# Every second forward substitution on POOL, and the two heads of a pair alternating in scores and chunk products

## The chip, the cores and the metric

The kernel runs on one core of a Trainium2 chip. Its engines are TensorE (PE: matrix products, PEld its weight loads), VectorE (DVE), ScalarE (ACT), GpSimd (POOL) and SyncE (SP), which here only issues transfers. Each engine takes its own instructions in the order in which the program put them down; between engines, semaphores make an instruction wait for what it reads and for buffers to come free. The metric is the device time of one execution in microseconds (us), lower is better; an execution with a profile gives the trace.

## The reference

One inference step of a hybrid decoder layer, for a prompt of 512 positions and, with the same weights, 8 single-token samples with caches. All is float32, the model width is 1024.

```python
proj = h @ w_in                        # h: RMS norm of x
# attention: 3 groups of 8 heads of 64, windows (128,1) (512,4) (2048,16): rotary q, k,
#   scores of 128-row blocks against 128 or 256 keys, masked softmax, times v,
#   groups weighted by the softmax of their log-sum-exp -> o_a
# RWKV-7 time mixing: 16 heads of 64, state S (64 x 64) carried over the 512 positions
def step(S, inp):
    r_t, w_t, k_t, v_t, kk_t, a_t = inp
    sa = einsum('bhij,bhj->bhi', S, -kk_t)
    S = S * w_t + sa * (kk_t * a_t) + v_t * k_t
    return S, einsum('bhij,bhj->bhi', S, r_t)
# group norm, bonus, gate -> o_b
merged = sigmoid(gate_a) * (o_a @ w_proj_a) + sigmoid(gate_b) * (o_b @ w_proj_b)
x = x + merged @ w_out
x = x + (silu(hn @ w_gate) * (hn @ w_up)) @ w_down
y = rms_norm(x)
```

The outputs are y for prompt and samples, the new keys and values, the new shift columns and the new states.

## The kernel before

**Layout and main stream.** Columns are the 512 prompt positions and the 8 samples, 520 in all, computed in two parts of 260. Every dense projection is a list of output tiles of 128 rows; a weight tile is split into a high and a low part (`whi` by ScalarE, `wlo` by VectorE), and each step of the inner dimension is three products, high times high, low times high and high times low, into a bank of accumulators called `mm` (three buffers). The main stream plays these tiles in the order input projections, gates, `w_proj_a`, `w_proj_b`, `w_out`, gate and up, down.

**Side work.** Beside it run generators, which the program calls the weave: attention `heads(g)` for each group, and for each of the eight pairs of RWKV heads `pair(p)`, `solve(p)`, a turn, `chain(p)`, `back(p)`. They take their accumulators from three buffers `ax` (`bank()`) and two single ones `ch0` and `ch1` (`cbank(i)`). `BANK` and `CBANK(i)` give the moment at which the next of them is expected to be free. A generator yields what must be ready before it can go on, and flags (`wv.set`, `wv.until`) order generators among each other.

**What sets the order.** The order is fixed when the program is built. `Clocks` keeps a planned time for each engine, and `Unit.price` gives each instruction a price: for VectorE 0.07 us plus n/960, for POOL 0.25 us plus n/480, where n is the number of elements per partition; a dependent instruction on the same engine starts 0.12 us later. Whenever the planned clock has passed what a generator waits for, its next piece is put into the engines' queues, otherwise dense tiles are. Every recorded instruction stands at line 380, the call in `Unit`, so the profile is read by tile names.

**Scores.** `heads(g)` goes through four pairs of heads. A pair's queries and keys lie in one tile, the first head in partitions 0 to 63, the second in 64 to 127. Before, the first head's blocks are multiplied into one `ch` bank after the other, each bank emptied by VectorE into `sm`, and then the second head's.

**Chunk products.** `pair(p)` cuts the 512 positions into 8 chunks of 64 and multiplies, for each head, the stacked tiles `BK` and `AR` of a chunk (contraction over the 64 rows of that head). Four chunks of one head fill an `ax` bank, VectorE multiplies it with a mask into `GH`, and in the second half POOL scales a part of it with `DN`.

**Forward substitution.** `solve(p)` inverts the unit triangular 32 by 32 blocks of a pair: two transfers bring them into `LT` (128 x 31 x 32), `Xs` (tile `X`, 128 x 8 x 32) starts as ones on the diagonal, and then there are 31 steps of two instructions, `xt = X * LT` and `X = X + xt`, in which the number of elements goes from 31 up to 76 and down to 8. `LT` and `X` have two buffers (`SOLVERS`), `xt` has one; every three steps (`SOLVE`) the generator yields. Two more transfers take the result back into `GH`, products on TensorE complete it to blocks of 64, and the flag `solved` lets the turn and the chain of that pair go on. The chain of pair p writes the state `o_wkvp` and gives `back(p)` what it needs for the tile `OB` that `w_proj_b` reads. `pb_pre(n)` and `pb_post(n)` are what goes before and after tile n of that projection.

Of the kernel before, what the change touches and what calls it, by code (L numbers as in the profile page):

```python
# [8 lines left out]
FP = mybir.dt.float32  # L9
# [3 lines left out]
ALU = mybir.AluOpType  # L13
# [12 lines left out]
NP = HB // 2  # L26
# [195 lines left out]
def _bc(ap, shape):  # L222
    return ap.to_broadcast(shape)
# [86 lines left out]
class Pool:  # L310
# [10 lines left out]
        h.append(t.name)  # L321
        return t

    def next(self, tag, bufs):

        h = self.hist.get(tag, ())
        return self.ck.free(h[-bufs], "PE") if len(h) >= bufs else 0.0


class Unit:  # L330
# [135 lines left out]
def program(tc, I, O):  # L466
    nc = tc.nc
    ck = Clocks()
    V, S, G, SY = (Unit(n, e, tc, ck) for n, e in (("DVE", nc.vector), ("ACT", nc.scalar), ("POOL", nc.gpsimd), ("SP", nc.sync)))

    E = Unit("PE", nc.tensor, tc, ck, tc.keep_in_program_order if PIN else None)
# [5 lines left out]
    def nm(s):  # L477
        uid[0] += 1
        return f"{s}_{uid[0]}"
# [16 lines left out]
    def bank():  # L496
        return axp.tile([128, 512], FP, name=nm("ax"), tag="ax", bufs=3)

    def cbank(i):
        return chp.tile([128, 512], FP, name=nm("ch"), tag=f"ch{i % 2}")  # L500

    def BANK():
        return axp.next("ax", 3)

    def CBANK(i):
        return lambda: chp.next(f"ch{i % 2}", 1)
# [310 lines left out]
    def heads(g):  # L817
# [2 lines left out]
        nb = 7 if g == 0 else 4  # L820
        kw = 256 if g == 0 else 128
        per = 512 // kw
        nb_ = 0
        for hp in range(4):
            for i in range(2):
                yield from wv.until("qk", g, i, hp)
            yield from wv.until("vt", g, hp)
            yield Q[hp], K[hp]
            PT = bp.tile([128, 2, 7, 128], FP, name=nm("PT"), tag="PT")
            sms = []  # L830
            for h2 in range(2):
                h = 2 * hp + h2
                r0 = h2 * 64
                q, k = Q[hp][r0:r0 + 64], K[hp][r0:r0 + 64]
                sm = bp.tile([128, 4, kw], FP, name=nm("sm"), tag="sm", bufs=2)
                nmx = bp.tile([128, 4], FP, name=nm("nmx"), tag="nmx", bufs=4)
                for b0 in range(0, 4, per):
                    nb_ += 1
                    yield (CBANK(nb_),)
                    ps = cbank(nb_)  # L840
                    for b in range(b0, b0 + per):
                        o = (b - b0) * kw
                        qb = q[:, b * 128:b * 128 + 128]
                        if g:
                            E.matmul(ps[:, o:o + 128], lhsT=qb, rhs=k[:, b * 128:b * 128 + 128], start=True, stop=True)
                        elif b:
                            E.matmul(ps[:, o:o + 256], lhsT=qb, rhs=k[:, (b - 1) * 128:(b + 1) * 128], start=True, stop=True)
                        else:
                            E.matmul(ps[:, o + 128:o + 256], lhsT=qb, rhs=k[:, 0:128], start=True, stop=True)
                    for b in range(b0, b0 + per):  # L850
                        o = (b - b0) * kw
                        lo = 128 if g == 0 and b == 0 else 0
                        m0 = (lo, 256, 384)[g]
                        V.tensor_tensor_reduce(out=sm[:, b, lo:], in0=ps[:, o + lo:o + kw],
                                               in1=amask[:, m0:m0 + kw - lo], scale=1.0, scalar=-3.0e38,
                                               op0=ALU.add, op1=ALU.max, accum_out=stat[:, g, 0, b, h:h + 1])
                V.tensor_scalar_mul(out=nmx[:], in0=stat[:, g, 0, :, h], scalar1=-0.125)
                for b in range(4):
                    lo = 128 if (g == 0 and b == 0) else 0
                    S.activation(out=sm[:, b, lo:], in_=sm[:, b, lo:], func=AF.Exp, scale=0.125,  # L860
                                 bias=nmx[:, b:b + 1], accum_out=stat[:, g, 1, b, h:h + 1])
                sms.append(sm)
            blks = ([(0, 128)] + [(b, o) for b in range(1, 4) for o in (0, 128)]) if g == 0 else \
                [(b, 0) for b in range(4)]
            for h2 in range(2):
# [266 lines left out]
    def pair(p):  # L1132
# [73 lines left out]

        GH = [r2.tile([128, NC, 2 * C], FP, name=nm("GH"), tag=tag, bufs=4) for tag in ("GB", "GK")]
        for c0 in range(0, NC, 4):
            for h in range(2):
                yield (BANK,)  # L1210
                ps = bank()
                for c in range(c0, c0 + 4):
                    E.matmul(ps[:, (c - c0) * 128:(c - c0 + 1) * 128], lhsT=BK[H[h], c, h:h + 2].rearrange("p a t -> p (a t)"),
                             rhs=AR[H[h], :, c], start=True, stop=True)
                V.tensor_tensor(out=GH[h][:, c0:c0 + 4], in0=ps[:].rearrange("p (c x) -> p c x", c=4),
                                in1=_bc(wmask[:].unsqueeze(1), [128, 4, 128]), op=ALU.mult)
                if c0:
                    G.tensor_tensor(out=GH[h][H[h], :, 0:C], in0=GH[h][H[h], :, 0:C],
                                    in1=_bc(DN[H[h]].unsqueeze(2), [64, NC, C]), op=ALU.mult)
# [54 lines left out]

    def solve(p):
        r2, QI, GH = rw["r2"], rw["QI"], rw["GH", p]
        TD = drp.tile([4, NC, 32, 32], FP, name=nm("TD"))
        TE = drp.tile([4, NC, 32, 32], FP, name=nm("TE"))
        for q in range(4):
# [4 lines left out]

        LT = r2.tile([128, 31, 32], FP, name=nm("LT"), tag="LT", bufs=SOLVERS)
        Xs = r2.tile([128, 8, 32], FP, name=nm("X"), tag="X", bufs=SOLVERS)
        V.memset(Xs[:], 0.0)
        for a in range(4):
            V.memset(Xs[a * 32:a * 32 + 32].rearrange("p m t -> p (m t)")[:, a:256:36], 1.0)
        yield (TD,)  # L1290
        for a in range(4):
            SY.dma_start(out=LT[a * 32:a * 32 + 32], in_=TD[:, :, :31].rearrange("q c s t -> (q c) s t"))
# [1 line left out]
        for s in range(31):  # L1294
            m = s // 4 + 1
            w = 31 - s
            t = r2.tile([128, 128], FP, name=nm("xt"), tag="xt")
            tv = t[:, :m * w].rearrange("p (m w) -> p m w", m=m)
            V.tensor_tensor(out=tv, in0=_bc(Xs[:, :m, s:s + 1], [128, m, w]),
                            in1=_bc(LT[:, s:s + 1, s + 1:], [128, m, w]), op=ALU.mult)  # L1300
            V.tensor_tensor(out=Xs[:, :m, s + 1:], in0=Xs[:, :m, s + 1:], in1=tv, op=ALU.add)
            if s % SOLVE == SOLVE - 1:
                yield (Xs,)
        yield (Xs,)
# [384 lines left out]
    def pb_pre(n):  # L1689
        def pre():  # L1690
            if n == 0:
                yield from wv.until("ob", NP - 3)
                hctx.close()
                mp = mrg["pool"] = pool("mg", mctx, side="right")
                mrg["h"] = mp.tile([128, KD, NT], FR, name="mh")
                mrg["l"] = mp.tile([128, KD, NT], FR, name="ml")
            gb = gp_.tile([128, NT], FP, name=nm("gb"), tag="g", bufs=2)
            ta = full("tmp", 2)
            G.dma_start(out=gb[:], in_=GD[:, KD + n])
            G.dma_start(out=ta[:], in_=TAD[:, n])  # L1700
            mrg[n] = gb, ta
            yield ()
        return pre
# [264 lines left out]
```

## Time and profile before

| | before |
|---|---|
| median of 3 runs | 1312.92 us (1310.77 to 1315.44) |
| the profiled execution | 1316.53 us, span 1314.8 us |
| mean granted TensorE clock | 0.983 |
| busy: TensorE, VectorE, ScalarE, POOL | 1264.7, 843.7, 610.6, 175.0 us |
| instructions: TensorE, VectorE, ScalarE, POOL | 11738, 2221, 1554, 261 |
| the substitutions' 496 instructions on VectorE | 60.3 + 57.6 us |
| first and last of them | 383.6 and 745.3 us |

A row of groups reads: line, engine, operation, output and inputs by tile names, shape and count, then the busy time, the mean of one in ns, and the idle time of the engine just before, with what ended it. A float32 product of the scores or chunks shows as two records of TensorE. A row of the windows view has a stretch, its length, the busy time of each engine with the number of instructions, then the granted TensorE clock, the share of the transfer engines and GB/s.

### The profile page before, as it was taken

How to read it: one execution, taken by the hardware profiler on the slowest of the kernel's cores; microseconds unless marked ns; L12 is line 12 of the kernel's file. 1: busy time of each engine (PE TensorE's matmuls, PEld its weight loads, DVE VectorE, ACT ScalarE, POOL GpSimd, SP SyncE). 2: the span in 40 equal slices, each digit the busy share in tenths (PEclk: the TensorE clock that was granted, in tenths of full speed). 3: DMA queues.
4: the chain of work that ended last, by engine and by line, in shares of the span. 5: the costliest groups of instructions: out<-in, count | busy, mean ns of one | idle time of the engine just before them, and what ended most of it. 6: DMA issues, size and time to landing. Idle time of an engine off the chain costs nothing.

```text
span 1314.8 us, 29468 instructions
## 1 busy us (share of the span) xinstructions
PE 1264.7 (96%) x11738; PEld 1197.5 (91%) x11738; DVE 843.7 (64%) x2221; ACT 610.6 (46%) x1554; POOL 175.0 (13%) x261
## 2 busy tenths in 40 slices
PE   7999999999989989999999999999999999999996
PEld 7998999989978878888888888999999999999996
DVE  6956866954869998886986665555843444332333
ACT  5244244366656656675785665334433232222220
POOL 1300100100223332121123122110200000000000
PEclk9999999999989999997999999999999999999998
DMA  6523654634245554543245454552222222223331
GB/s 215 158 94 96 213 178 146 221 112 172 69 131 136 152 147 141 143 156 97 77 139 168 123 175 157 182 192 85 81 97 97 97 89 89 97 93 89 89 101 65
DMA packets 92137, 169.48 MB, mean 129 GB/s; under 512 B 42416, under 2 KB 47568, under 8 KB 92000
## 3 DMA queue, kind: packets, MB, share of 16 engines
q1 hardware_dynamic: 60880, 102.46, 24.6%
q0 software_dynamic: 14512, 46.47, 11.5%
q10 hardware_dynamic: 16608, 18.68, 4.3%
q8 instruction: 92, 1.51, 0.5%
q14 instruction: 45, 0.37, 0.1%
HBM read 133.20 MB, written 27.94 MB: 123 GB/s over the span
## 4 chain that ended last, share of the span: by engine, by line
PE 64%; DVE 15%; issue 9%; DMA 6%; ACT 4%; POOL 1%; SPq 1%; ACTq 0%; DVEq 0%; POOLq 0%
PE mm L380 51%; PE ax L380 8%; PE ch L380 5%; DVE wlo L380 2%; DVE X L380 1%; DVE xt L380 1%; DMA fb<-FD 1%; DMA sw<-raw 1%; ACT KB L380 1%; DVE k L380 1%; DMA raw<-w_in 1%; SPq L380 1%; DVE raw L380 1%; DVE qk L380 1%; DVE GH L380 1%
## 5 line engine op out<-in xcount | busy, mean ns | idle before, releaser
L380 PE MATMUL mm<-hh,whi 128*128 128x260 f32 x1136 | 340.2, 299 | 0.8 <-ACT gt L380 0.8
L380 PE MATMUL mm<-hh,wlo 128*128 128x260 f32 x1136 | 325.4, 286 | 4.3 <-DVE wlo L380 4.3
L380 PE MATMUL mm<-hl,whi 128*128 128x260 f32 x1136 | 325.7, 287 | 0.0
L380 ACT CAST whi<-raw 128x1024 fp32r<-128x1024 f32 (+1 forms) x165 | 170.1, 1032 | 324.4 <-PE mm L380 290.6
L380 DVE TENSOR_TENSOR wlo<-raw,whi 128x1024 fp32r<-128x1024 f32 (+1 forms) x165 | 197.9, 1199 | 140.2 <-ACT whi L380 137.0
L380 PEld LDWEIGHTS mm<-hh,whi 128*128 128x128 f32 x1136 | 215.7, 190 | 13.3 <-issue 6.0
L380 PEld LDWEIGHTS mm<-hh,wlo 128*128 128x128 f32 x1136 | 215.4, 190 | 6.5 <-DVE wlo L380 5.8
L380 PEld LDWEIGHTS mm<-hl,whi 128*128 128x128 f32 x1136 | 215.5, 190 | 1.4 <-issue 0.2
L380 PE MATMUL mm<-h2l,whi 128*128 128x260 f32 x608 | 171.5, 282 | 0.0
L380 PE MATMUL mm<-h2h,wlo 128*128 128x260 f32 x608 | 171.4, 282 | 0.0
L380 PE MATMUL mm<-h2h,whi 128*128 128x260 f32 x608 | 171.4, 282 | 0.0
L380 PEld LDWEIGHTS mm<-h2h,wlo 128*128 128x128 f32 x608 | 114.5, 188 | 0.0
L380 PEld LDWEIGHTS mm<-h2l,whi 128*128 128x128 f32 x608 | 114.4, 188 | 0.0
L380 PEld LDWEIGHTS mm<-h2h,whi 128*128 128x128 f32 x608 | 114.4, 188 | 0.0
L380 PE MATMUL mm<-fh,wlo 128*128 128x260 f32 x388 | 109.6, 282 | 0.0
L380 PE MATMUL mm<-fh,whi 128*128 128x260 f32 x388 | 109.5, 282 | 0.0
L380 PE MATMUL mm<-fl,whi 128*128 128x260 f32 x388 | 109.5, 282 | 0.0
L380 PEld LDWEIGHTS mm<-fh,whi 128*128 128x128 f32 x388 | 73.1, 188 | 0.0
L380 PEld LDWEIGHTS mm<-fl,whi 128*128 128x128 f32 x388 | 73.0, 188 | 0.0
L380 PEld LDWEIGHTS mm<-fh,wlo 128*128 128x128 f32 x388 | 72.9, 188 | 0.0
L380 DVE TENSOR_TENSOR xt<-X,LT 128x60 f32<-128x60 f32 (+24 forms) x248 | 60.3, 243 | 3.6
L380 DVE TENSOR_TENSOR X<-X,xt 128x60 f32<-128x60 f32 (+24 forms) x248 | 57.6, 232 | 3.8
(390 smaller groups left out, 2588.8 us busy)
## 6 DMA issues: line engine op xcount, KB each, us to landing
raw<-w_in SPq DMA_DIRECT2D x77, 512.0 KB, 3.7
raw<-w_gate SPq DMA_DIRECT2D x22, 512.0 KB, 3.2
raw<-w_up SPq DMA_DIRECT2D x22, 512.0 KB, 3.2
raw<-w_down SPq DMA_DIRECT2D x16, 512.0 KB, 3.5
kt<-kcache POOLq DMA_DIRECT2D x24, 256.0 KB, 3.7
kt<-vcache POOLq DMA_DIRECT2D x24, 256.0 KB, 3.5
sw<-raw ACTq DMA_DIRECT2D x64, 65.0 KB, 3.6
GD<-gt ACTq DMA_DIRECT2D x16, 260.0 KB, 3.0
```

The source lines that it names most:

```text
L380: r = f(*a, **k)
```

## The change

In `solve(p)` the four lines that compute on `X` use a name `B`, which is VectorE for even p and POOL for odd p: the five memsets and all 62 instructions of the steps of pairs 1, 3, 5 and 7. In `heads(g)` the two heads of a pair are multiplied block by block in turn, head 0 into `ch0` and head 1 into `ch1`; both banks must be free before, and both are emptied after. In `pair(p)` the chunk products of the two heads alternate in the same way into two `ax` banks, which are taken together (`BANK2`). `pb_pre(1)` awaits the flag of the last pair's chain.

```diff
-    def next(self, tag, bufs):
+    def next(self, tag, bufs, i=0):
         h = self.hist.get(tag, ())
-        return self.ck.free(h[-bufs], "PE") if len(h) >= bufs else 0.0
+        return self.ck.free(h[i - bufs], "PE") if len(h) >= bufs - i else 0.0
...
+    def BANK2():
+        return max(BANK(), BANK(1))
...
-            for h2 in range(2):
-                h = 2 * hp + h2
...
-                for b0 in range(0, 4, per):
-                    nb_ += 1
-                    yield (CBANK(nb_),)
-                    ps = cbank(nb_)
-                    for b in range(b0, b0 + per):
-                        o = (b - b0) * kw
+            for b0 in range(0, 4, per):
+                yield CBANK(0), CBANK(1)
+                pss = [cbank(0), cbank(1)]
+                for b in range(b0, b0 + per):
+                    o = (b - b0) * kw
+                    for h2 in range(2):
+                        q, k, ps = Q[hp][H[h2]], K[hp][H[h2]], pss[h2]
...
+                for h2 in range(2):
+                    h = 2 * hp + h2
                     for b in range(b0, b0 + per):
...
         for c0 in range(0, NC, 4):
+            yield (BANK2,)
+            pss = [bank(), bank()]
+            for c in range(c0, c0 + 4):
+                for h in range(2):
+                    E.matmul(pss[h][:, (c - c0) * 128:(c - c0 + 1) * 128], lhsT=BK[H[h], c, h:h + 2].rearrange("p a t -> p (a t)"),
+                             rhs=AR[H[h], :, c], start=True, stop=True)
             for h in range(2):
-                yield (BANK,)
-                ps = bank()
-                for c in range(c0, c0 + 4):
-                    E.matmul(ps[:, (c - c0) * 128:(c - c0 + 1) * 128], lhsT=BK[H[h], c, h:h + 2].rearrange("p a t -> p (a t)"),
-                             rhs=AR[H[h], :, c], start=True, stop=True)
-                V.tensor_tensor(out=GH[h][:, c0:c0 + 4], in0=ps[:].rearrange("p (c x) -> p c x", c=4),
+                V.tensor_tensor(out=GH[h][:, c0:c0 + 4], in0=pss[h][:].rearrange("p (c x) -> p c x", c=4),
...
     def solve(p):
+        B = (V, G)[p % 2]
...
-        V.memset(Xs[:], 0.0)
+        B.memset(Xs[:], 0.0)
...
-            V.tensor_tensor(out=tv, in0=_bc(Xs[:, :m, s:s + 1], [128, m, w]),
+            B.tensor_tensor(out=tv, in0=_bc(Xs[:, :m, s:s + 1], [128, m, w]),
...
-            V.tensor_tensor(out=Xs[:, :m, s + 1:], in0=Xs[:, :m, s + 1:], in1=tv, op=ALU.add)
+            B.tensor_tensor(out=Xs[:, :m, s + 1:], in0=Xs[:, :m, s + 1:], in1=tv, op=ALU.add)
...
     def pb_pre(n):
+            if n == 1:
+                yield from wv.until("chain", NP - 1)
```

How the rows move. On TensorE, the first pair of heads of group 0 (`ch` are the score banks, `qk` the tile of queries or keys, `mm` a dense tile):

```order
 L380 MATMUL ax_905<-ident,raw_874 128x128 x4
-L380 MATMUL ch_914<-qk_652,qk_415 128x128
-L380 MATMUL ch_914<-qk_652,qk_415 128x256
-L380 MATMUL ch_919<-qk_652,qk_415 128x256 x2
+L380 MATMUL ch_916<-qk_652,qk_415 128x128
+L380 MATMUL ch_917<-qk_652,qk_415 128x128
+L380 MATMUL ch_916<-qk_652,qk_415 128x256
+L380 MATMUL ch_917<-qk_652,qk_415 128x256
 L380 MATMUL mm_886<-hh,whi_823 128x260
```

Before, the first head's four blocks went into two banks in a row; now two blocks of each head go in turn into two banks, and the other two blocks follow after dense rows.

On POOL, the middle of the last pair's substitution (pair 7, `X_9810`), as it now stands:

```order
L380 TENSOR_TENSOR xt_10393<-X_9810,LT_9809 128x66
L380 TENSOR_TENSOR X_9810<-X_9810,xt_10393 128x6x11
L380 TENSOR_TENSOR svd_10218<-uk,sel 48x256
L380 DMA o_wkvs<-st_9951 128x512
L380 DMA tmp_11079<-OBD 128x512
L380 DMA br_10442<-GTD 128x512
L380 DMA tmp_11163<-OBD 128x512
L380 DMA OBD<-KB_7392 128x512
L380 DMA bvr_10669<-BVD 128x512
L380 TENSOR_TENSOR xt_10460<-X_9810,LT_9809 128x60
L380 TENSOR_TENSOR X_9810<-X_9810,xt_10460 128x6x10
```

Before, POOL's queue held only the `svd` products and the transfers at this place. Now the substitution's steps stand in it, with these nine rows, one `svd` of them further up, among their 62.

On VectorE, part of an even pair's substitution (`X_5720`) in the changed program, with what each row waits for:

```order
L380 TENSOR_TENSOR xt_5874<-X_5720,LT_5719 128x29 [waits DVE_49]
L380 SCALAR_TENSOR_TENSOR k_5942<-pb_5941,mu,k_5942 128x511 [waits Activation_49]
L380 TENSOR_TENSOR X_5720<-X_5720,xt_5874 128x29 [waits DVE_49]
L380 SCALAR_TENSOR_TENSOR k_5942<-shift,mu,k_5942 128x8
L380 TENSOR_SCALAR sg_6361<-k_5942,feat 128x8 [waits DVE_49]
L380 TENSOR_TENSOR xt_5997<-X_5720,LT_5719 128x28 [waits Pool_49]
L380 TENSOR_TENSOR X_5720<-X_5720,xt_5997 128x28 [waits DVE_49]
L380 TENSOR_TENSOR xt_6000<-X_5720,LT_5719 128x54 [waits DVE_49]
```

The fourth step's `xt` now waits for POOL, whose steps use the same buffer `xt`; before, all steps of all pairs ran on VectorE and none had such a wait.

More of the change, by code (lines that the diff above doesn't have):

```diff
@@ L500, in cbank, with BANK @@
         return chp.tile([128, 512], FP, name=nm("ch"), tag=f"ch{i % 2}")
-    def BANK():
-        return axp.next("ax", 3)
+    def BANK(i=0):
+        return axp.next("ax", 3, i)
+    def BANK2():
+        return max(BANK(), BANK(1))
     def CBANK(i):
@@ L822, in heads @@
         per = 512 // kw
-        nb_ = 0
         for hp in range(4):
@@ L829, in heads @@
             PT = bp.tile([128, 2, 7, 128], FP, name=nm("PT"), tag="PT")
-            sms = []
+            sms, nmxs = [], []
             for h2 in range(2):
-                h = 2 * hp + h2
[L833 to L836, printed above, removed]
-                for b0 in range(0, 4, per):
-                    nb_ += 1
-                    yield (CBANK(nb_),)
-                    ps = cbank(nb_)
-                    for b in range(b0, b0 + per):
-                        o = (b - b0) * kw
+                sms.append(bp.tile([128, 4, kw], FP, name=nm("sm"), tag="sm", bufs=2))
+                nmxs.append(bp.tile([128, 4], FP, name=nm("nmx"), tag="nmx", bufs=4))
+            for b0 in range(0, 4, per):
[5 more added lines that the diff above has]
+                        q, k, ps = Q[hp][H[h2]], K[hp][H[h2]], pss[h2]
                         qb = q[:, b * 128:b * 128 + 128]
@@ L853, in heads @@
                         m0 = (lo, 256, 384)[g]
-                        V.tensor_tensor_reduce(out=sm[:, b, lo:], in0=ps[:, o + lo:o + kw],
+                        V.tensor_tensor_reduce(out=sms[h2][:, b, lo:], in0=pss[h2][:, o + lo:o + kw],
                                                in1=amask[:, m0:m0 + kw - lo], scale=1.0, scalar=-3.0e38,
                                                op0=ALU.add, op1=ALU.max, accum_out=stat[:, g, 0, b, h:h + 1])
+            for h2 in range(2):
+                h, sm, nmx = 2 * hp + h2, sms[h2], nmxs[h2]
                 V.tensor_scalar_mul(out=nmx[:], in0=stat[:, g, 0, :, h], scalar1=-0.125)
@@ L861, in heads @@
                                  bias=nmx[:, b:b + 1], accum_out=stat[:, g, 1, b, h:h + 1])
-                sms.append(sm)
             blks = ([(0, 128)] + [(b, o) for b in range(1, 4) for o in (0, 128)]) if g == 0 else \
@@ L1286, in solve @@
         Xs = r2.tile([128, 8, 32], FP, name=nm("X"), tag="X", bufs=SOLVERS)
-        V.memset(Xs[:], 0.0)
+        B.memset(Xs[:], 0.0)
         for a in range(4):
-            V.memset(Xs[a * 32:a * 32 + 32].rearrange("p m t -> p (m t)")[:, a:256:36], 1.0)
+            B.memset(Xs[a * 32:a * 32 + 32].rearrange("p m t -> p (m t)")[:, a:256:36], 1.0)
         yield (TD,)
```

## The prediction

> **What bounds the kernel now.** I read the page first: the busy shares of the engines, then the slices, then the shares of the chain that ended last.
>
> ```profile
> span 1314.8 us, 29468 instructions
> PE 1264.7 (96%) x11738; PEld 1197.5 (91%) x11738; DVE 843.7 (64%) x2221; ACT 610.6 (46%) x1554; POOL 175.0 (13%) x261
> DVE  6956866954869998886986665555843444332333
> PEclk9999999999989999997999999999999999999998
> PE 64%; DVE 15%; issue 9%; DMA 6%; ACT 4%; POOL 1%; SPq 1%; ACTq 0%; DVEq 0%; POOLq 0%
> ```
>
> TensorE is busy 96% of the span, but the chain is TensorE's for only 64%: in the middle the chain passes through VectorE, transfers and bare issue. So I cut the span into stages with the windows view, and asked it once for the substitution's tile `xt` alone (third row below: its first three columns are VectorE, ScalarE and POOL).
>
> ```profile
> core 0: us, PE busy (x) PEld busy (x) DVE busy (x) ACT busy (x) POOL busy (x), PEclk, DMA share, GB/s
> 350.00:830.00 480.00, 454.61 (x5015) 406.75 (x5014) 381.53 (x1251) 303.17 (x908) 117.41 (x170) 0.97 0.47 138
> 350.00:830.00 480.00, 117.96 (x496) 0.00 (x0) 0.00 (x0) 0.97 0.47 138
> 721.00:746.00 25.00, 25.00 (x341) 21.07 (x339) 19.94 (x85) 13.94 (x52) 4.38 (x7) 1.00 0.37 108
> 746.00:810.00 64.00, 61.03 (x792) 52.94 (x791) 37.21 (x117) 45.13 (x167) 14.11 (x27) 1.00 0.52 166
> 850.00:1300.00 450.00, 449.73 (x3769) 449.06 (x3769) 199.27 (x309) 128.97 (x183) 14.18 (x18) 1.00 0.30 99
> L380 ACTq DMA_DIRECT2D o_wkvp<-last x8: 338/344/345, 540.0 to 808.9; - x8
> 745.27 0.17 DVE L380 TENSOR_TENSOR X<-X,xt 128x8 f32<-128x8 f32 x1
> ```
>
> From 850 on TensorE never stops: that stage is dense projections and nothing in the change touches it. All eight substitutions lie in 350 to 830, where TensorE stands still for 480 − 454.6 = 25.4 us and VectorE is busy 381.5 of 480. The last substitution ends at 745 and the last pair's chain at 809, with 505 us of work behind it until the span's end. **The question is therefore when the last pair's chain ends.** Dense work fills TensorE up to there (61.0 of 64 us in 746 to 810), so either side can set it: too much TensorE work ahead of it, or a substitution that arrives late, with TensorE's order fixed at build time and nothing left to slip in.
>
> **The change part by part.** The sum is made against the profiled execution, 1316.5 us, 3.6 over the median of the runs shown.
>
> *Two heads alternating on TensorE.*
>
> ```profile
> L380 PE MATMUL ax<-AR,BK 64*128 64x128 f32 x256 | 34.8, 313 | 2.4 <-ACT VTr L380 1.9 <-DVE GH L380 0.4
> L380 PE MATMUL ch<-qk,qk 64*128 64x128 f32 x144 | 19.1, 291 | 0.0
> L380 PE MATMUL ch<-qk,qk 64*128 64x256 f32 x48 | 12.5, 383 | 0.0
> L380 PE MATMUL ax<-GH,AT 64*64 64x64 f32 x224 | 8.5, 221 | 0.0
> 346.88 2.26 PE L380 MATMUL ax<-AR,BK 64*128 64x128 f32 x24
> ```
>
> The chunk products cost 34.8/256 = 136 ns each, the scores 19.1/144 = 133 ns, or 12.5/48 = 260 ns at twice the columns. The fourth row is a product in which the heads already alternate, each on its own half of the rows: 8.5/224 = 38 ns for 64 columns, so 76 per 128. At that price the scores (144 + 2 × 48 = 240 units) cost 18.2 instead of 31.6: −13.4. The last row shows that three banks of chunk products in a run, where the head changes from bank to bank, cost 2.26/24 = 94 ns already; I take the alternating ones at that: 256 × (136 − 94) = −10.8. Sum **−24**. Ends: 0, if what makes the 64*64 group cheap is that its heads also write different column halves, and −33, half of all three groups.
>
> *Four substitutions leave VectorE.* 117.96/496 = 238 ns an instruction, 62 for each pair: 14.7 us a pair, 59 for the four odd ones. What does such an instruction cost on POOL? The trace has none of this size; the nearest are these, and the first row shows what they do to VectorE.
>
> ```profile
> 701.82 1.07 DVE L380 TENSOR_TENSOR xt<-X,LT 128x70 f32<-128x70 f32 x1
> 703.91 0.22 DVE L380 TENSOR_TENSOR xt<-X,LT 128x65 f32<-128x65 f32 x1
> 700.21 0.68 DVE L380 TENSOR_TENSOR GH<-ax,wmask 128x512 f32<-128x512 f32 x1
> 700.16 2.64 POOL L380 TENSOR_TENSOR GH<-GH,DN 64x512 f32<-64x512 f32 x2
> 513.99 1.04 POOL L380 TENSOR_TENSOR st<-st,sg 128x512 f32<-128x512 f32 x1 [10.06 <-PE ax L380]
> 621.20 0.61 POOL L380 TENSOR_TENSOR svd<-uk,sel 48x256 f32<-48x256 f32 x1 [10.61 <-ACT uk L380]
> L1960 POOL MEMSET const-float32-1.0<- 128x1 f32 x1 | 0.1, 103 | 0.0
> ```
>
> The straight line through 0.61 us at 256 columns and 1.04 at 512 is 0.18 + 0.00168 n. A step's instruction has 50 columns on average (1560 over 31 steps, from the loop's bounds), so **0.26 us**, an estimate between 0.10 (the memset) and 0.61 (the nearest product). That is 62 × 0.26 = 16.4 us a pair, 65 for four. During a POOL instruction VectorE does not run one with two inputs from the on-chip buffer: the substitution's step took 1.07 us beside POOL's 2.64 and 0.22 once that had ended at 702.80, while a product that reads an accumulator (third row) took its usual 0.68. So VectorE is relieved of 59 us and held for up to 65: **0**. The lower end is what TensorE loses to VectorE in this stage at all. The waits view of TensorE there has eleven rows that name VectorE, 14.7 us together, the first being
>
> ```profile
> PE mm L380 <- DVE wlo L380: 3.3, 4, 1.4
> ```
>
> so −15, and as much again for +15. The Trainium skill, "SBUF — State Buffer", section "SBUF: two separate sides", calls this port pair an exclusive lock, held for the whole instruction, against which a VectorE instruction with two SBUF inputs blocks. By that rule the offload frees nothing, as entered; without it the sum would be 15 lower. The rows above (1.07 against 0.22) agree with it.
>
> *The odd substitutions take longer from end to end.* Steps depend on each other, so one pair's 62 instructions run one after the other, and POOL's queue is in order: what stands between them is waited for. In the last pair these are two `svd` products and seven transfers, with the waits that POOL shows in the window of the last substitution (busy, mean, then idle before):
>
> ```profile
> L380 POOL TENSOR_TENSOR svd<-uk,sel 48x256 f32<-48x256 f32 x2 | 1.2, 606 | 6.2 <-ACT uk L380 3.5 <-PE ax L380 2.7
> L380 POOL DMA_DIRECT2D ga<-GD x2 | 1.1, 558 | 1.7 <-DVE X L380 1.6
> L380 POOL TENSOR_TENSOR st<-st,sg 128x512 f32<-128x512 f32 x1 | 1.0, 1038 | 6.4 <-PE ax L380 6.4
> L380 POOL DMA_DIRECT2D o_wkvs<-st x1 | 0.6, 585 | 4.3 <-DVE X L380 4.3
> L380 POOL DMA_DIRECT2D st<-swkv x1 | 0.5, 538 | 3.1 <-DMA o_wkvs<-st 3.1
> ```
>
> The instructions alone: 62 × (0.26 + 0.04 between them, as VectorE shows) = 18.6. The port: VectorE without the odd steps is busy (381.5 − 59)/480 = 67%, its mean instruction is 381.5/1251 = 0.305 us, so each POOL step waits 0.67 × 0.15 us: 6.2. The nine others in the queue: 2 × 0.61 + 7 × 0.55 = 5.1. Their own waits: 21.7 us stand in the rows above; part of these belongs to work outside the steps, I take 8. Together **38 us**, against 24 (721 to 745) on VectorE. The order on TensorE was built with a price for POOL of 0.25 + n/480 and 0.12 between steps, 62 × 0.47 = 29, so even where the build made room, 9 us are not covered. The last pair's +14 falls straight on the last chain. Of the other three's 42 I count half, 21, since other pairs' work lies between. Both engines' steps share the one `xt` buffer, so where an even and an odd substitution overlap, three steps of the one wait for three of the other; for pairs 1 to 3 I add 4. Sum **+39**. Ends: +10 (the last pair alone, without its queue's waits) and +87 (0.61 us for each instruction: 62 × 0.65 + 19 = 59 us a pair, +35 for the last, 52 for the others).
>
> *The clock.* The clock row is low in two slices only:
>
> ```profile
> 362.00:394.00 32.00, 26.18 (x229) 24.16 (x228) 21.27 (x50) 18.04 (x46) 8.95 (x13) 0.89 0.41 128
> 592.00:625.00 33.00, 31.76 (x269) 28.38 (x269) 21.76 (x80) 17.87 (x47) 5.31 (x7) 0.74 0.30 93
> ```
>
> These cost 0.11 × 32 = 3.5 and 0.26 × 33 = 8.6 us, around a stretch of 5.8 us of stall in the first. With 39 us of new stalls on top of 25.4 I count two more such drops: **+12** (0 to +24). The Trainium skill, "TensorE: Matmul & The Clock Gate", section "Part 1: The HAM clock gate (the "warmup" mystery)", lowers the clock after about 3.4 us of idleness; if the new stalls stay shorter than that, this term is 0 and the sum would be 12 lower. The second row, with 1.2 us of idle time in 33, shows a low clock without such a stall.
>
> *At nothing:* the scores now need both of their banks at once, so a pair of heads waits until the four evacuations of the second bank are done too,
>
> ```profile
> L380 DVE CUSTOM_DVE_ANT_0 sm<-ch,amask x96: 275/286/426, 72.0 to 326.8; 128x128 f32<-128x128 f32 x72, 128x256 f32<-128x256 f32 x24
> ```
>
> 4 × 0.286 = 1.1 us; in the built order some 24 dense rows stand between one such pair of banks and the next, so they hide it, and uncovered it would be 1.1 us at each of 16 places. Also the memsets that go along (five per pair, ahead of the loads), and the wait for the last chain in `pb_pre` of the second tile: in the built order that projection already stands behind the last chain's rows, and its own matmuls need the chain's result. If that cover were gone it would hold up two small loads.
>
> Sum: 1316.5 − 24 + 0 + 39 + 12 = 1343.5; less 3.6 for the median, **1340 us**.
>
> **The rivals.** *A, the solves stay hidden: faster, 1289.* The last substitution had 24 us, 0.77 per step of two instructions. If a step on POOL stays under that, waits included, nothing arrives later and only the −24 is left: 1316.5 − 24 − 3.6. For it: the two instructions alone are 0.60. Against it: 0.17 a step is all that remains for the port and for the queue, which hold 19 us over 31 steps, 0.62. *B, the parts cancel: 1313.* Only the last pair's +14 and half of the others' 21 come through, against −24. For it: TensorE did not stand at all during the last substitution (25.00 of 25.00 us in 721 to 746), so dense work covered the whole of it. Against it: that work is in a fixed order, and what now covers 24 us was laid out for 29. *C, POOL's small instructions are dear: 1392.* At 0.61 each the latency term is +87, the clock +12 and the coupling +4 more: 1316.5 − 24 + 87 + 12 + 4 − 3.6. For it: 0.61 is the nearest measured product. Against it: it has five times the columns, and the memset shows that 0.10 is possible. Should alternating heads save nothing, the forecast becomes 1364, which I count with C.
>
> **How the numbers follow.** A difference under about 0.3%, 4 us, can't be told from none. Forecast 0.54, with its own range 1318 to 1365; A 0.19, B 0.10, C 0.17. Faster: all of A and 0.02 of B, 0.21; within 0.3%: half of B, 0.05; slower: the rest, 0.74. The range runs from 1290, where half of A still lies inside, to 1385, with half of C.
>
> **What would show it.** Right: the last chain's state transfer near 836 instead of 809; an odd substitution of 35 to 40 us; POOL instructions of its steps near 0.26 us; VectorE's busy time in the middle no lower by more than a few us although 248 instructions are gone, its two-input ones being longer; scores and chunk products near 80 to 95 ns per 128 columns; 850 to the end unchanged but later. Wrong in the first part: the products still at 130. Wrong in the third: the last substitution no longer than 24 us, or TensorE's idle time in the middle not above 35 us. The prediction falls if the last chain ends before 809.

## The result: 3.4% slower

The changed kernel takes 1357.14 us (median of 4 runs, 1354.65 to 1359.16) against 1311.85 us for the kernel before, measured beside it. The ratio is 1.0343, with an interval of 1.031 to 1.0377: 45 us slower. The forecast was slower, 1340 us, with a range of 1290 to 1385.

The page of the changed kernel, its profiled execution 1359.16 us:

```profile
span 1357.4 us, 29467 instructions
PE 1277.5 (94%) x11738; PEld 1201.2 (88%) x11738; DVE 799.4 (59%) x1953; ACT 610.4 (45%) x1554; POOL 271.7 (20%) x529
DVE  6958958845699666767547354455764444432234
PEclk9999999999989889789889999999999999999998
PE 56%; issue 14%; DVE 11%; POOL 8%; DMA 8%; ACT 1%; SPq 1%; ACTq 0%; DVEq 0%; POOLq 0%
```

VectorE lost 843.7 − 799.4 = 44 us of work and POOL gained 97, and POOL, 1% of the chain before, is now 8% of it. The clock row, low in two slices of the middle before, is now low in seven of the ten from the 12th to the 21st.

The same stretch of both kernels, from 350 us until both last chains have ended (windows view, first before, then changed), and the last chain's state transfer of the changed kernel:

```profile
350.00:870.00 520.00, 493.95 (x5338) 445.47 (x5337) 404.42 (x1287) 314.79 (x922) 124.39 (x183) 0.97 0.47 141
```

```profile
350.00:870.00 520.00, 467.54 (x4957) 412.63 (x4956) 334.12 (x981) 302.61 (x905) 211.97 (x432) 0.91 0.43 125
870.00:1340.00 470.00, 469.04 (x3924) 467.74 (x3923) 208.36 (x322) 135.01 (x190) 18.02 (x25) 1.00 0.31 102
L380 ACTq DMA_DIRECT2D o_wkvp<-last x8: 338/344/345, 525.7 to 848.1; - x8
```

The transfer moved from 808.9 to 848.1, 39 us, and after that TensorE is full as before: the loss lies where the prediction looked for it. TensorE stands 52.5 us in the stretch instead of 26.1, and the clock lost 0.09 × 520 = 47 us instead of 0.03 × 520 = 16. So some 26 us more idle time and up to 31 more of clock (this counts the low clock also where TensorE stands) are set against the work saved on TensorE, whose groups are:

```profile
L380 PE MATMUL ax<-AR,BK 64*128 64x128 f32 x256 | 24.7, 314 | 1.6 <-DVE BK L380 1.1 <-DVE GH L380 0.4
L380 PE MATMUL ch<-qk,qk 64*128 64x128 f32 x144 | 14.0, 297 | 0.0
L380 PE MATMUL ch<-qk,qk 64*128 64x256 f32 x48 | 7.5, 396 | 0.1
```

24.7/256 = 96 ns for a chunk product (136 before), 14.0/144 = 97 for a score (133 before), together 46.2 instead of 66.4 us. By these groups the saving of 20 us is there, and yet the kernel is slower.

The substitution on POOL, first as groups (busy, mean ns, idle time before), then the smallest, median and largest duration, and then the break in the last pair's:

```profile
L380 POOL TENSOR_TENSOR xt<-X,LT 128x60 f32<-128x60 f32 (+24 forms) x124 | 47.0, 379 | 22.3 <-DVE X L380 12.9 <-DVE DN L380 0.7 <-DVE ys L380 0.4
L380 POOL TENSOR_TENSOR X<-X,xt 128x60 f32<-128x60 f32 (+24 forms) x124 | 46.5, 375 | 9.1
...
L380 POOL TENSOR_TENSOR xt<-X,LT x124: 202/294/1314, 413.8 to 793.6; 128x60 f32<-128x60 f32 x12, 128x28 f32<-128x28 f32 x8, 128x54 f32<-128x54 f32 x8, 128x48 f32<-128x48 f32 x8
...
746.05 0.24 POOL L380 TENSOR_TENSOR xt<-X,LT 128x31 f32<-128x31 f32 x1
763.40 0.31 POOL L380 TENSOR_TENSOR X<-X,xt 128x66 f32<-128x66 f32 x1
765.78 0.58 POOL L380 DMA_DIRECT2D o_wkvs<-st  x1 [1.51 <-DVE st L380]
776.13 0.54 POOL L380 DMA_DIRECT2D tmp<-OBD  x1 [9.76 <-DVE OB L380]
785.74 0.29 POOL L380 TENSOR_TENSOR xt<-X,LT 128x60 f32<-128x60 f32 x1 [0.40 <-DVE ys L380]
793.88 0.21 POOL L380 TENSOR_TENSOR X<-X,xt 128x8 f32<-128x8 f32 x1
```

An instruction of a step takes 0.2 to 0.33 us undisturbed and 0.377 on average. The four odd substitutions, from first to last instruction, take 82, 81, 30 and 48 us; on VectorE before, the starts and ends, paired in order, give 72, 46, 61 and 31. The last pair's 62 run from 746.05 to 794.1, 48 us: 21 steps in 17.7 us, then 22 us in which POOL's queue goes through one product and six transfers (9.8 of it is a wait for a buffer that VectorE had to free), then ten steps in 8.4.

The chain of waits between 400 and 850 us, by line, before and changed:

```profile
by line: PE mm L380 28.4%; PE ax L380 12.3%; PE ch L380 10.2%; issue 7.3%; DVE X L380 3.0%; DVE wlo L380 2.9%; DVE xt L380 2.7%; ACT KB L380 2.3%; DMA fb<-FD 1.9%; DMA kt<-vcache 1.7%; DMA tmp<-OBD 1.6%; ACT gq L380 1.5%; DMA tmp<-OAD 1.5%;
```

```profile
by line: PE mm L380 22.9%; issue 12.3%; PE ax L380 8.6%; POOL X L380 8.5%; POOL xt L380 8.4%; PE ch L380 7.8%; DMA fb<-FD 3.8%; DMA OBD<-KB 2.6%; DMA br<-GTD 2.5%; DMA o_wkvs<-st 2.2%; DMA tmp<-OBD 1.5%; DVE xt L380 1.3%; DMA TE<-X 1.2%; AC
```

Before, the substitutions' steps hold 5.7% of these 450 us, 26 us, all on VectorE. Now POOL's alone hold 16.9%, 76 us. That is 50 us more on the chain. Transfers that POOL issues (`fb`, `kt`, `tmp`, `OBD`, `br`, `o_wkvs`) show 12.6% in this row against 6.7% in the one before.

### The profile page after: what moved, and what is told of

Same layout as the page of the kernel before. It is cut to its first block, busy times and chain, and to the rows that moved or that the text cites. A ratio compares the mean times of both kernels' runs of the same rounds, so it can differ in the third digit from the quotient of the medians.

```text
span 1357.4 us, 29467 instructions
## 1 busy us (share of the span) xinstructions
PE 1277.5 (94%) x11738; PEld 1201.2 (88%) x11738; DVE 799.4 (59%) x1953; ACT 610.4 (45%) x1554; POOL 271.7 (20%) x529
## 3 DMA queue, kind: packets, MB, share of 16 engines
q1 hardware_dynamic: 60880, 102.46, 24.3%
## 4 chain that ended last, share of the span: by engine, by line
PE 56%; issue 14%; DVE 11%; POOL 8%; DMA 8%; ACT 1%; SPq 1%; ACTq 0%; DVEq 0%; POOLq 0%
PE mm L380 47%; PE ax L380 6%; PE ch L380 4%; POOL X L380 3%; POOL xt L380 3%; DMA fb<-FD 2%; DVE wlo L380 1%; SPq L380 1%; POOL kt L380 1%; DMA OBD<-KB 1%; DMA br<-GTD 1%; DMA o_wkvs<-st 1%; DVE xt L380 1%; DMA raw<-w_in 1%; DVE raw L380 1%
## 5 line engine op out<-in xcount | busy, mean ns | idle before, releaser
L380 PE MATMUL mm<-hh,whi 128*128 128x260 f32 x1136 | 345.7, 304 | 4.0 <-ACT v L380 4.0
L380 PE MATMUL mm<-hh,wlo 128*128 128x260 f32 x1136 | 332.5, 293 | 6.8 <-DVE wlo L380 6.6
L380 PE MATMUL mm<-hl,whi 128*128 128x260 f32 x1136 | 331.7, 292 | 0.0
L380 PEld LDWEIGHTS mm<-hh,whi 128*128 128x128 f32 x1136 | 220.7, 194 | 16.6 <-issue 5.3
L380 PEld LDWEIGHTS mm<-hh,wlo 128*128 128x128 f32 x1136 | 220.4, 194 | 9.8 <-DVE wlo L380 7.9
L380 PEld LDWEIGHTS mm<-hl,whi 128*128 128x128 f32 x1136 | 220.8, 194 | 2.0 <-issue 0.3
L380 ACT ACTIVATE GH<-ch,DN 64x64 f32<-64x64 f32 x128 | 39.5, 308 | 39.8 <-PE ch L380 34.8
L380 POOL TENSOR_TENSOR xt<-X,LT 128x60 f32<-128x60 f32 (+24 forms) x124 | 47.0, 379 | 22.3 <-DVE X L380 12.9
```

The lines of the kernel that those rows point to most:

```text
L380: r = f(*a, **k)
```

## The experiments

The theory: the terms of the sum add, TensorE's saving is worth its 20 us and POOL's slower substitutions cost more than that. The rivals: the saving is worth nothing since TensorE isn't what the end waits for; the loss comes from the order that was built with POOL's prices; from POOL's queue; from the shared `xt` buffer; from the port that POOL and VectorE share (a VectorE step of 0.22 us took 1.07 beside a POOL product, as the prediction's rows show).

**Each part alone.** First the alternation alone, with `B = V` for all pairs:

```diff
-        B = (V, G)[p % 2]
+        B = V
```

> All substitutions stay on VectorE; scores and chunk products alternate as in the change. Terms add (the prediction's view): the saving on TensorE stands alone, 10 us on the scores and 10 on the chunk products by the trace of the change, so 1312 - 20 = 1292 us (1286 to 1300), and the last chain's state transfer comes near 789 us instead of 809. Rival, the chain through VectorE sets the time, not TensorE's work: 1312 within 4, transfer at 809 within 5. Rival, alternating disturbs the order: 1318 or more, with more idle time on TensorE between 350 and 830 than the 25.4 us before.

Measured: 1320.39 us, ratio 1.0059 (1.0027 to 1.009). This is no gain but a small loss. Windows view of the kernel before and, below it, of this one:

```profile
350.00:850.00 500.00, 473.95 (x5170) 425.47 (x5169) 392.87 (x1270) 309.43 (x916) 121.26 (x178) 0.97 0.47 139
```

```profile
350.00:850.00 500.00, 467.53 (x5147) 416.78 (x5146) 386.75 (x1266) 308.55 (x914) 119.69 (x177) 0.97 0.47 138
```

TensorE worked 6.4 us less there and stood as much longer. Over the whole span, by the pages, its busy time fell from 1264.7 to 1253.1, so by 11.6 and not by the 20 of the groups, and its idle time rose from 50.1 to 60.3. The saving turns into idle time. (The profiled execution took 1315.23 us, one of the faster of ten; the last chain's transfer came at 806.0, against 808.9 before.) Then the odd substitutions on POOL alone, with scores and products as before:

```diff
+        B = (V, G)[p % 2]
...
-            V.tensor_tensor(out=tv, ...
+            B.tensor_tensor(out=tv, ...
```

> Only the odd substitutions move to POOL; scores and products as before. Terms add: 1357 + 20 = 1377 us (1370 to 1385). Rival, TensorE's saving is lost in the change because the chain sets the time: 1357 within 5. Granted clock between 350 and 870 near 0.91, as in the change, by both; if it is back at 0.97 the clock loss belongs to the alternation.

Measured: 1359.66 us, 1.0345 (1.0301 to 1.0388), within 3 us of the whole change. So POOL costs 47 us over the 1312.40 beside it, and the alternation is worth 2.5 at most in the change. The clock loss belongs to POOL's part:

```profile
350.00:850.00 500.00, 452.89 (x4779) 400.51 (x4778) 324.75 (x962) 292.71 (x888) 203.72 (x431) 0.92 0.44 127
```

Its page has TensorE busy 1284.6 of 1358.2 us. Against the kernel before this is 23.5 us more idle time and 19.9 us more for the same matmuls at the lower clock.

**Each alternation alone**, in the kernel before, and both with the planner told of the new price:

```diff
+    EH = Unit("PE", nc.tensor, tc, ck, tc.keep_in_program_order if PIN else None)
+    EH.price = lambda op, outs, ins: 0.7 * E.price(op, outs, ins)
...
-                    E.matmul(pss[h][:, (c - c0) * 128:(c - c0 + 1) * 128], ...
+                    EH.matmul(pss[h][:, (c - c0) * 128:(c - c0 + 1) * 128], ...
```

> The kernel before with the scores' alternation alone. Terms add: 10 us less on TensorE, 1302. Found so far: both alternations together took 10.6 us of TensorE's busy time away up to 850 us and TensorE stood 10.6 us longer, and the time rose by 0.6%. If the two banks that must be free together hurt, this kernel is slower than before (1316 or more) and the products' kernel is not; if the saving is only idle time elsewhere, 1312 within 4.

> The kernel before with the chunk products' alternation alone. Terms add: 10 to 12 us less on TensorE, 1301. If the saving turns into idle time since the chain sets the end: 1312 within 4. If taking two of the three ax banks at once hurts: 1316 or more.

> Both alternations, substitutions on VectorE, and the planner is told that the alternating products cost 0.7 of its old price (96 of 136 ns measured). If the saving was lost because the order was laid out for the old durations: 1300 or less. If the chain through the other engines sets the time: no better than the 1320 of the same kernel without this, within 6.

Measured: scores alone 1312.05 us, 0.9993 (0.9975 to 1.001); products alone 1313.50, 1.0003 (0.9984 to 1.0021); both, priced, 1312.47, 0.9992 (0.9966 to 1.0018). None differs from the kernel before, though the alternated groups take 10 to 12 us less in each (TensorE's whole busy time fell by 7.4 with the scores and by 1.0 with the products, which ran at a clock of 0.979 on average against 0.983). Taking two banks at once does no harm by itself, and the kernel with the right price shows no loss but no gain either. In these orders TensorE's saving is worth nothing.

**The order or the engine.** The change's plan, POOL's prices included, but the odd substitutions' instructions issued on VectorE. The order is nearly the change's; in the traces about 8% of TensorE's rows stand at another place, since moved instructions shift their neighbours:

```diff
+    GV = Unit("POOL", nc.vector, tc, ck)
...
-        B = (V, G)[p % 2]
+        B = (V, GV)[p % 2]
```

> The program of the change, planned with POOL's prices for the odd substitutions, so in nearly its order, but these instructions are issued on VectorE. If POOL itself is the cause (its slower instructions and its queue, which held the last substitution for 22 us): near the kernel that only alternates, about 1295 us. If the order that was built with POOL's prices is the cause: 1340 or more, with the same idle time on TensorE as in the change (52 us from 350 to 870).

Measured: 1327.95 us, 1.0112 (1.0082 to 1.0142), between the two forecasts. Over the 1320 of the alternation alone the order that was laid out for POOL costs 8; the engine that carries the instructions costs 1357 − 1328 = 29.

**Which pairs.** The last pair back on VectorE:

```diff
-        B = (V, G)[p % 2]
+        B = (V, G)[p % 2 and p < NP - 1]
```

> The change, but the last pair's substitution is on VectorE again; pairs 1, 3 and 5 on POOL. If the last pair's own substitution (48 us on POOL, 30 on VectorE before) carries the loss: 1357 - 18 = 1339 us or less, as the 22 us stop in POOL's queue goes too (about 1335). If the earlier ones carry it (pair 3 ended 47 us late, pair 7 began 31 us late): 1350 to 1357.

Measured: 1345.38 us, 1.0237 (1.0182 to 1.0293). The last pair is worth 12 us, and pairs 1, 3 and 5 the other 25 over the alternation alone. Both answers hold in part; the earlier pairs together carry twice as much, although other pairs' work follows them.

**The shared buffer.** POOL's steps, all but the first, write their products into rows of `LT` that are used up:

```diff
-            t = r2.tile([128, 128], FP, name=nm("xt"), tag="xt")
+            if p % 2 and s:
+                t = LT[:].rearrange("p s t -> p (s t)")
+            else:
+                t = r2.tile([128, 128], FP, name=nm("xt"), tag="xt")
```

> The change, but the odd substitutions write their step's products into rows of LT that are used up (all steps but the first), so VectorE's and POOL's substitutions no longer wait for each other on the one xt buffer. The prediction priced this coupling at 4 us: 1357 - 4 = 1353 (1348 to 1357). Rival, the coupling is what stretched the first two POOL substitutions to 80 us each and made pair 3 end 47 us late: 1340 or less.

Measured: 1354.66 us, 1.0324 (1.029 to 1.0357). 2.5 us less than the change, inside what the medians can vary: the coupling is not the cause, with the reservation that about an eighth of TensorE's rows moved as well. The trace says more. First and last instruction of the first two odd substitutions:

```profile
411.19 0.24 POOL L380 TENSOR_TENSOR xt<-X,LT 128x31 f32<-128x31 f32 x1
440.71 0.21 POOL L380 TENSOR_TENSOR X<-X,LT 128x8 f32<-128x8 f32 x1
508.75 0.23 POOL L380 TENSOR_TENSOR xt<-X,LT 128x31 f32<-128x31 f32 x1 [4.29 <-DVE X L380]
538.09 0.21 POOL L380 TENSOR_TENSOR X<-X,LT 128x8 f32<-128x8 f32 x1
```

They take 30 us each instead of 82 and 81, the other two 30 and 33. None is more than 3 us longer than the shortest odd one on VectorE before, and the kernel is still 44 us slower than the 1310.31 beside it. The last chain's transfer comes at 832.5, 16 us earlier than in the change, and that too bought only the 2.5. So the length of an odd substitution from end to end isn't what costs. What this trace shows instead is the reverse side of POOL's queue, a product that stands behind the steps:

```profile
438.01 0.61 POOL L380 TENSOR_TENSOR svd<-uk,sel 48x256 f32<-48x256 f32 x1
438.67 1.22 PE L380 MATMUL ax<-svd,uk 48*128 48x256 f32 x2 [12.27 <-POOL svd L380]
```

POOL reaches this `svd` without a pause after 54 instructions of the substitution's 62, and TensorE stands 12.27 us for it. All its waits for `svd` from 350 to 850 are 15.3 us here, 3.9 in the change and 0.6 in the kernel before.

**POOL's queue.** Thirteen kinds of transfers are issued by SP, in the change and, as a control, in the kernel that only alternates:

```diff
-        G.dma_start(out=O["o_wkvs"][p], in_=st[:])
+        SY.dma_start(out=O["o_wkvs"][p], in_=st[:])
...
-                G.dma_start(out=t[:, :T], in_=OBD[:, i])
+                SY.dma_start(out=t[:, :T], in_=OBD[:, i])
```

> The change, but thirteen kinds of transfers of this stage (outputs and inputs of the attention merge, the sample states, the normalised pair outputs) are issued by SP instead of POOL; the last substitution then has no foreign row between its steps. If POOL's queue, which stood 22 us in the last substitution, carries the loss of that pair: the last substitution takes 24 to 26 us instead of 48 and the time falls by about 12, what the last pair was worth (1357 to 1345), or more if it held the earlier ones too: 1335 to 1345. If the instructions themselves and the port carry it: 1355 or more. To be read against the kernel that only alternates with the same transfers moved.

> Control: all substitutions on VectorE, heads alternate, the same thirteen kinds of transfers issued by SP. If the move itself is neutral: 1320 within 5. If SP's queue suffers (weights are late): 1330 or more, and this difference is taken off the other run's.

Measured: 1347.03 us with POOL's substitutions, 1.0233 (1.0173 to 1.0294), and 1300.94 without, 0.9916 (0.9889 to 0.9943). The break in the last substitution is gone, it takes 34 us (721.1 to 754.9) instead of 48 and ends when the control's does (753.8). Still POOL costs 46 us over its control, as much as before (its four runs lie between 1335.9 and 1357.6, so this is 46 give or take 8). So the transfers in the queue lengthened one substitution but don't carry the loss. Windows view of the two, the one with POOL first:

```profile
350.00:850.00 500.00, 457.28 (x4899) 403.94 (x4898) 328.81 (x977) 299.02 (x903) 150.52 (x329) 0.91 0.44 128
650.00:700.00 50.00, 44.58 (x406) 37.62 (x407) 30.04 (x92) 26.89 (x88) 14.82 (x32) 0.77 0.38 110
```

```profile
350.00:850.00 500.00, 480.96 (x5276) 429.80 (x5275) 386.01 (x1278) 315.22 (x919) 67.07 (x80) 0.98 0.49 144
```

By the pages the two profiled executions differ by 45.7 us: TensorE stands 69.4 instead of 45.1 us, 24.3 more, and its busy time is 21.4 longer for the same matmuls. The second row shows a stretch at 0.77 in which TensorE stood only 5.4 of 50 us. But the stall behind it began ahead of the window:

```profile
645.00:650.00 5.00, 0.00 (x0) 0.00 (x0) 0.00 (x0) 0.00 (x0) 3.98 (x14) 0.51 0.00 0
652.91 0.61 POOL L380 TENSOR_TENSOR svd<-uk,sel 48x256 f32<-48x256 f32 x1
653.58 1.22 PE L380 MATMUL ax<-svd,uk 48*128 48x256 f32 x2 [10.75 <-POOL svd L380]
690.00:702.00 12.00, 12.00 (x50) 9.53 (x50) 6.96 (x23) 2.71 (x7) 3.71 (x8) 0.50 0.42 108
```

TensorE stood 10.75 us, from 642.8 on, for an `svd` that POOL again reached only after 54 of a substitution's 62 instructions, and the clock fell to half within this stall. So this run took the transfers out of POOL's queue, but not the products behind the steps. The low clock from 690 on, with no idle time, follows a stall of only 1.85 us.

The control is faster than both kernels, so its transfers were also moved in the kernel before, with nothing else changed.

> The kernel before with only the thirteen kinds of transfers moved from POOL to SP. If the 1301 us of the alternating kernel with this move come from the transfers alone: 1301 within 4. If the saving of the alternation counts once the transfers are out of the way: 1310 or more here.

Measured: 1312.35 us, 1.0016 (0.9995 to 1.0037). The transfers alone bring nothing, the alternation alone nothing, both together 0.84%. Whether that is the saving that now counts, or an order that happened to turn out well, isn't settled by one order of each.

**The port.** On that control, POOL runs beside each odd step two products on constants that nobody reads; the substitutions stay on VectorE:

```diff
+            if p % 2:
+                dz, n = rw["xz"][:, 76:], min(m * w, 52)
+                nc.gpsimd.tensor_tensor(out=dz[:, :n], in0=ident[:, :n], in1=ident[:, :n], op=ALU.mult)
+                nc.gpsimd.tensor_tensor(out=dz[:, :n], in0=dz[:, :n], in1=ident[:, :n], op=ALU.add)
```

> The kernel that only alternates, with its transfers issued by SP (1301 us), and on POOL, beside each step of an odd substitution that VectorE does as before, two products of up to 52 columns on constants whose result nobody reads: 248 instructions in the same form and number as the change moves, in an order for TensorE that is the same but for some fifty rows. If the port that both engines share is what costs: 1330 to 1347. If the cost is that POOL's slower steps stand in the chain that others wait for: 1301 to 1311, and the wait for the port shows only as some longer VectorE instructions.

Measured: 1359.47 us, 1.0374 (1.0341 to 1.0408), 58 us over its control. The number is nearer to the port's forecast and above both. The trace shows another cause. Waits of TensorE, then POOL's added groups, then VectorE's own steps from 350 to 480 us, where both engines ran them, and the same of the control:

```profile
PE ax L380 <- POOL svd L380: 45.6, 3, 45.2
PE ax L380 <- DVE sg L380: 13.8, 2, 11.8
```

```profile
L1311 POOL TENSOR_TENSOR xt<-xt,ident 128x52 f32<-128x52 f32 (+12 forms) x124 | 43.2, 348 | 9.5
L1310 POOL TENSOR_TENSOR xt<-ident 128x52 f32<-128x52 f32 (+12 forms) x124 | 41.0, 331 | 9.4
```

```profile
L380 DVE TENSOR_TENSOR xt<-X,LT 128x28 f32<-128x28 f32 (+21 forms) x34 | 8.9, 260 | 0.3
L380 DVE TENSOR_TENSOR X<-X,xt 128x54 f32<-128x54 f32 (+21 forms) x33 | 8.8, 268 | 0.2
```

```profile
L380 DVE TENSOR_TENSOR X<-X,xt 128x54 f32<-128x54 f32 (+22 forms) x72 | 19.3, 268 | 0.7
L380 DVE TENSOR_TENSOR xt<-X,LT 128x54 f32<-128x54 f32 (+22 forms) x72 | 18.5, 257 | 0.7
```

The products, waiting for nothing, all ran early, between 353 and 462 us, and ahead of an `svd` product in POOL's queue; TensorE stood 45.2 us in one piece for that, and 11.8 once more. By the pages its idle time rose by 54 us, from 45.1 to 99.1. VectorE's steps took 260 and 268 ns beside them, 257 and 268 in the control, and its whole busy time was 834.1 us against 830.9. So the run tried the queue once more, not the port: for VectorE the port cost some 3 us, and 248 small instructions ahead of products that TensorE needs cost nearly all of the 58 us.

**What is shown and what is not.** Shown: POOL's part makes the loss (47 us alone; 29 for the engine alone in nearly the same order), the alternation is worth nothing in any of the orders but one, and neither the shared buffer (2.5), nor the transfers in POOL's queue (46 us remain without them), nor the last pair alone (12), nor the order built with POOL's prices (8), nor the length of the odd substitutions (30 to 33 us with the buffer apart, and no faster) carries it. What is left is what the steps do while they stand in POOL's queue: on the chain of waits they hold 76 us instead of 26, and products that TensorE needs stand behind them. In two runs this cost TensorE 12.3 and 10.8 us in one piece. In the change its direct waits for `svd` are only 3.9 us, and the rest of its idle time goes through VectorE and ScalarE; that it, too, comes from POOL's queue is argued from the chain. No run leaves the steps on POOL and moves the other products away, so how much of the 47 us this explains isn't known.

About half of the loss shows as longer busy time for the same matmuls, at the lower clock (20 of 43 us with POOL's part alone, 21 of 46 with the transfers moved). In the changed kernel each of the eleven drops of the clock between 350 and 850 us begins 1.8 to 3.6 us after the start of a stall of TensorE of 1.2 to 4.0 us; in other kernels some drops have no such stall. Why some last long after the stall (17 us from 571.8 on) stays open.

## Why the prediction was right, point by point

The direction held, the range, 95 us wide, held the time, and the forecast was 17 us short. What held of the mechanism is that the odd steps on POOL cost more, through waits and clock, than the alternation brings. The last chain did come later, by 39 us. But the reason entered for it, odd substitutions that take longer from end to end, isn't what the runs bear out; that the sum came so near is in part luck.

**Two heads alternating, −24: this term failed.** By the groups the size of the saving was nearly right (20 us; the chunk products 10.1 of 10.8, the scores 10.1 of 13.4), but TensorE's whole busy time fell by 11.6 only with the alternation alone, and the unalternated chunk products took 30.4 instead of 34.8 us in the kernel with the scores alone, so part of their 10.1 isn't the alternation's. What failed is the step from TensorE's work to time. The prediction said that either side can set when the last chain ends, and then entered the whole of both sides in one sum. The runs put the saving at 0 in the kernel before and at 2.5 in the change. With 0 in its place the sum is 1343.5 + 24 − 3.6 = 1364, 7 over the measured time.

**Four substitutions leave VectorE, 0.** The size was wrong and the entry right. An instruction costs POOL 0.377 us on average, not 0.26; undisturbed it is 0.20 at 8 columns and 0.33 at 76, near the estimate (0.19 and 0.31). The long ones coincide with VectorE's instructions of two inputs: the longest, 1.31 us from 755.75 on, with a `wlo` of 1.23 from 755.66 on, so I take the rest as waiting for the port. VectorE's remaining steps rose only from 243 and 232 ns to 258 and 248:

```profile
L380 DVE TENSOR_TENSOR xt<-X,LT 128x60 f32<-128x60 f32 (+24 forms) x124 | 32.0, 258 | 14.0 <-POOL X L380 12.7
L380 DVE TENSOR_TENSOR X<-X,xt 128x60 f32<-128x60 f32 (+24 forms) x124 | 30.7, 248 | 1.4
```

So of the 59 us relief VectorE kept 44, where the prediction had all of it eaten by the port. The rule of the Trainium skill ("SBUF — State Buffer", "SBUF: two separate sides") that the loser of the port blocks shows in single rows, but its cost fell mostly on POOL. The prediction expected VectorE's busy time to stay, and that was wrong; the 44 us bought no time.

**The odd substitutions take longer, +39.** By the runs POOL's part without the alternation's loss is 1357 − 1320 = 37 us, the clock included, or 47 alone. The division: 12 for the last pair (14 predicted), 25 for the others (21), 2.5 for the buffer (4). But the term was entered as the substitutions' length, and with the buffer apart they took 30 to 33 us, less in sum than on VectorE before, and the loss stayed. The pieces agree by luck as far as this goes. An odd substitution was to take 35 to 40 us and took 82, 81, 30 and 48. The last one took 48 us, not 38, with 22 us in the queue where 13 were counted, and before it had taken 30, not 24: 721 was where the window began, its first step is

```profile
714.73 0.19 DVE L380 TENSOR_TENSOR xt<-X,LT 128x31 f32<-128x31 f32 x1
```

And the run with the transfers moved shows that the stop in this one is not what costs.

**The clock, +12.** This was up to 31 us in the change's trace. Latency and clock together, 51 predicted, stand against 47 for POOL's part alone, so the sum of the two was good and the division wrong: there idle time on TensorE grew by 23.5, and the clock took nearly as much, 19.9, on top. By the rule of the Trainium skill named beside it ("TensorE: Matmul & The Clock Gate", "Part 1: The HAM clock gate (the "warmup" mystery)") the term would have been 0 with stalls under about 3.4 us. The changed kernel has several above that,

```profile
PE ax L380 <- DVE GH L380: 11.1, 4, 6.5
PE ch L380 <- ACT GH L380: 9.2, 3, 4.0
PE ax L380 <- ACT GH L380: 4.0, 1, 4.0
PE mm L380 <- ACT v L380: 4.0, 1, 4.0
```

while the longest wait of the kernel before in that stage was

```profile
PE ax L380 <- DVE sd L380: 3.2, 1, 3.2
592.82 0.33 PE L380 MATMUL ch<-VTr,GH 64*64 64x64 f32 x4 [1.45 <-DVE AR L380]
594.00:610.80 16.80, 16.80 (x100) 14.85 (x98) 10.61 (x29) 6.39 (x14) 4.70 (x6) 0.50 0.28 85
```

The direction agrees, the figure doesn't: with no stall over 3.2 us the kernel before lost its clock as well, here for 16.8 us in which TensorE didn't stand at all, behind a stall of 1.45 us. The measurement decides: short stalls cost clock too.

**At nothing.** The wait of the scores for both banks cost nothing in time (1312.05 with the scores alone).

**The rivals.** A, the solves stay hidden, had the condition of 0.77 us a step; with the true 30 us before it is 0.97, and between foreign rows POOL met it, 17.7/21 = 0.84, as did whole substitutions of 30 us in the run with the buffer apart. It was slower all the same, so the condition was not the one that decides. B fell with the size of the loss: 47 us for POOL's part is far from what a saving of 20 could cancel, even if it had counted. C's price of 0.61 us was not reached.

## What to carry to other kernels

Work taken off an engine need not shorten the time, even if the engine is busy 96% of it: here 10 to 20 us taken from its groups came to nothing in all orders but one. Before adding such a saving to a sum, ask which side is the later one, and don't enter both. A serial recurrence of small instructions on a second engine is to be priced by what stands behind it in that engine's queue and by what TensorE's stalls cost in clock, not by its own length or by the relief of the first engine: here 44 us of relief on VectorE came with 45 us of loss. A window of a profile can cut off the stall that explains it; look ahead of its edge. An experiment that adds dummy work has to be read in its trace, as such work may run at another place than the work it stands for.

## What the runs showed of the hardware

Two products on different halves of the rows, each into its own bank, overlap: 89 to 97 ns per 128 columns in turn (114 for the chunk products with POOL's steps and the transfers moved) against 119 to 136 in a row. When POOL ran many small two-input instructions beside VectorE, it was mostly POOL that waited: single ones of its steps took up to 1.31 us, beside a VectorE instruction of 1.23, where 0.33 is undisturbed, while VectorE's mean stayed within 3 ns in the run with the added products. In the stretch 350 to 850 the granted clock was 0.96 to 0.98 in the kernels whose TensorE stood 19 to 32 us there, and 0.91 to 0.93 in those, all with work added on POOL, where it stood 43 to 72 us. At the fine scale it was half or whole: 0.50 from 594.0 to 610.8 us in the kernel before, with TensorE busy throughout.
